# Last joins sooner, first values in two pieces, four decays moved to ScalarE, one transpose moved behind a product

## The chip, the cores and the metric

The kernel runs on one core of a Trainium2 chip. The metric is device time in microseconds (us), the median of three runs. A profiled execution gives a trace besides: every instruction of every engine with its start and duration, and every transfer. TensorE (PE) multiplies matrices, VectorE (DVE), ScalarE (ACT) and GpSimd (POOL) work element by element, SyncE (SP) issues most transfers (DMAs), ACT some. Each engine works through its own list of instructions in order and waits at semaphores for the others.

## The reference

Two layers over 512 latent tokens and 256 context tokens, width 1024: a bidirectional gated delta rule (16 value heads, 8 key heads, chunks of 64 tokens), then attention. The change touches the first layer. Cut to what matters there:

```
kb, vb = kc * bc[..., None], vc * bc[..., None]
a = where(strict, einsum('bhncd,bhnsd->bhncs', kb, kc) * decay, 0)
t_inv = triangular_solve(eye + a, eye, lower=True, unit_diagonal=True)
u = einsum('bhncs,bhnse->bhnce', t_inv, vb)
w = einsum('bhncs,bhnsd->bhncd', t_inv, kb * exp(gc)[..., None])
qk = einsum('bhncd,bhnsd->bhncs', qc, kc) * decay
...
def step(s, xs):                                  # over the chunks, in order
    v_new = u_i - einsum('bhcd,bhde->bhce', w_i, s)
    o = einsum('bhcd,bhde->bhce', qd_i, s) + einsum('bhcs,bhse->bhce', qk_i, v_new)
    s = s * gl_i + einsum('bhcd,bhce->bhde', kd_i, v_new)
    return s, o
...
def finish(o, z):                                 # after the scan
    o = rms_norm(transpose(o, (0, 2, 1, 3)), o_norm_g)
    return (o.reshape(b, l, DN_VAL_DIM) * silu(z)) @ w_out
```

## The kernel before, in words

The tokens lie in six tiles of 128 (t = 0 to 5); a tile holds one chunk for the forward and the mirrored chunk for the backward direction. Three stages matter here.

**Projection stage** (about 140 to 550 us). For each of 40 heads of q, v and z (order `qzzqq...vvzvzvvzzz`: the last are v14, v15, z13, z14, z15) TensorE multiplies in two pieces, 512 and 256 tokens wide (`g512_v15`, `g256_v15`; 24 products each, line 929). A v head is then convolved and gated (VectorE lines 944 and 963), turned by TensorE (`tr_v15`, 461), copied by ScalarE (`vt15`, 994) and stored to memory (`v_d`, 995). Beside it the triangular inverses are made, two tiles at a time: GpSimd solves a 32-wide system column by column (`X0`, `X1`, `X2`, lines 812 and 813), the result is weighed by beta (`weigh`, 817; for the last pair on VectorE), VectorE turns it (`U_4`, `U_5`, 831), and then the halves of each tile are joined: TensorE `pp` (`j_first`, 840), ScalarE `pn` (846), TensorE `pw` (`j_second`, 864), ScalarE copies into `Tt` (852, 871), store to `t_d` (855).

The order of all this on PE, ACT, DVE, POOL and SP is set by a planner (`written_out`): each `Piece` has an engine, a cost, a due time, the pieces it comes after, and the buffers it takes. A piece may start once what it waits for has ended plus a margin (3 us on PE, or the piece's own `slack`); the one that could start first is taken next.

**Recurrence** (about 550 to 730 us). 12 steps (s) of four groups of four heads (p), x = 4s + p. Per x: `ks` (state times keys and queries, 1560), `r` (1563), `pr` (T times r, 1586), `vn` (copy of it, ACT 1588), `vd` (`vn` times a decay, one instruction per head, 1596 on VectorE in step 0, 1598 on ScalarE later), `pq` (1612), `su` (1620), and on VectorE the new state `S` (1632 in step 0, 1634 later) and output `O`. Step 0 starts from a zero state, so it has no `ks`; its `r` is the values tile `cv_0` itself. `pr`, `pq` and `su` have one PSUM buffer each, `ks` two. Each step's tiles (`ck`, `cq`, `cv`, `cT`, `cQK`, `ckt`) are loaded by SP, for step 0 within the projection stage (`first_matrices`, `first_values`). SP's transfers and ACT's share eight semaphores in turn: a transfer is issued only when the eighth before it has landed.

**Output heads** (from about 730 us). Units n = 0 to 31, two groups of three tiles for each of 16 heads: `so` (scaled output, ACT 1690), `pt` (turned, TensorE 1697), gated by z (DVE 1706), `y0` (rounded, ACT 1713) and `y1` (the rest, DVE 1719), product `po` with the split weights (1740). Unit 0 is started within the last x: its third tile (`C`) is turned at x = 47.

Of the kernel before, what the change touches and what calls it, by code (L numbers as in the profile page):

```python
# [86 lines left out]
def backbone(tc, a, out):  # L87
# [713 lines left out]
    def solve_steps(pair):  # L801

        def clear():
            X = Xs[pair] = room["tp" if pair else "even"].tile([P, 2, 32, 32], F32, tag="CDB"[pair], name=f"X{pair}")
            G.memset(X, 0.0)
            G.memset(raw(X.rearrange("p t i j -> p (t i j)"), 0, [[1024, 2], [33, 32]]), 1.0)

        def column(j):
            n, L, X = 31 - j, Ls[pair], Xs[pair]
            tmp = room["tp"].tile([P, 512], F32, tag="tmp", name=f"tmp{j}_{pair}")  # L810
            tv = tmp[:, 0:2 * n * (j + 1)].rearrange("p (t i k) -> p t i k", t=2, i=n)
            G.tensor_tensor(tv, bcast(L[:, :, j + 1:, j], 3, j + 1), bcast(X[:, :, j, 0:j + 1], 2, n), ALU.mult)  # L812
            G.tensor_tensor(X[:, :, j + 1:, 0:j + 1], X[:, :, j + 1:, 0:j + 1], tv, ALU.subtract)  # L813

        def weigh(i):
            X = Xs[pair][:, i]
            (V if pair in (2,) else G).tensor_tensor(X, X, bcast(bball[:, 2 * pair + i], 1, 32), ALU.mult)
# [212 lines left out]

    def first_values():
        opening["v"] = values_tile(0)
        values_loaded(0, opening["v"])

# [292 lines left out]
    for n, (c, h) in enumerate(heads):  # L1327
# [26 lines left out]
        if c == "v":  # L1354
            tu = Piece("PE", 0.6, t0 - 20, head_turned, n, after=si, takes=["tr", "tr"], holds=[("sil", sq_[0])], lands=0.1)
# [42 lines left out]
    for pair in range(3):  # L1398
        first = None
        for j, (cost, f_) in enumerate(solve_steps(pair)):  # L1400
            e = "DVE" if j > 31 and pair in (2,) else "POOL"
            x = Piece(e, 1.22 if e == "DVE" else cost, T0 + (460, 382, 316)[pair], f_, port=1 + (e == "POOL" and 0 < j < 32), after=[turned_["s", 2 * pair], turned_["s", 2 * pair + 1]] + prev, holds=[("L", turned_[2 * pair])] if j < 32 else [], lands=0.1)
            prev = [x]
        solved[pair] = x
    joined = []
    for t in range(NT):
# [4 lines left out]
        U[1].after.append(U[0])  # L1411
        pp = Piece("PE", 1.23, -20, j_first, t, after=U, takes=["gq"], holds=[(u, U[0]), ("mo", mo_of[t])], lands=0.1)
        ne = Piece("ACT", 0.7, due + 4, j_negative, t, after=[pp], takes=["pn"], holds=[("gq", pp)], lands=0.1)
        pw = Piece("PE", 1.23, -20, j_second, t, after=[ne], takes=["gq"], holds=[(u, U[0]), ("pn", ne)], lands=0.1)
        cs = [Piece("ACT", 1.25, due + 10, j_copies, t, b, after=U, takes=[f"Tt{t // 5}"] if b == 0 else (), holds=[(u, U[0])], lands=0.1) for b in range(4)]
# [87 lines left out]
    if True:  # L1503
# [71 lines left out]
        def solve(x):  # L1575
# [14 lines left out]
            if s < 11:  # L1590
                vd = ch.tile([P, 4, P], F32, tag="vd", name=f"vd{x}", bufs=2)
                for c in range(4):
                    h = 4 * p + c
                    el = (elX if c > 1 else elV)[:, visit, t, h:h + 1]
                    if s == 0:
                        V.tensor_scalar(vd[:, c], vn[:, c], el, None, ALU.mult)
# [156 lines left out]
    for x in range(50):  # L1753
# [143 lines left out]
    for n in range(32):  # L1897
# [20 lines left out]
        if n + 2 < 32:  # L1918
            gate_load(n + 2)
            out_scale(n + 2)  # L1920
        if n < 10:
# [632 lines left out]
```

## Time and profile before

| | |
|---|---|
| median of three runs | 1175.51 us (1174.72 to 1175.9) |
| profiled execution, its own time | 1170.3 us |
| its span, first to last instruction | 1168.5 us |
| mean granted TensorE clock | 0.991 |
| TensorE busy | 1124.7 us, 96% |
| VectorE, ScalarE, GpSimd busy | 69%, 62%, 50% |

In a timeline each row is a run of like instructions: start, duration in us, engine, source line, output and inputs, count; in brackets the idle time before it and what ended it. "issue" is idle time for which the profile shows no one that was waited for. Rows of queues (ACTq, SPq) are transfers being issued. A row of windows gives, for a stretch of time, busy time and instructions of each engine, then the granted clock of TensorE, the share of the transfer engines in use and their rate in GB/s. A matrix product of 32-bit values shows as two TensorE records for each one in the program.

### The profile page before, as it was taken

What the parts mean: (1) busy time and instruction counts of PE and PEld (TensorE: products, weight loads), DVE (VectorE), ACT (ScalarE), POOL (GpSimd) and SP (SyncE); (2) the same over time, 40 slices, a digit from 0 to 9 for tenths busy, and PEclk for the clock granted to TensorE, in tenths of its full rate; (3) what the DMA queues carried; (4) which work ended last, traced back from release to release, by engine and by line L of the source; (5) the groups of instructions that cost most, each with busy time, mean ns of one, the idle gap of its engine ahead of it and who ended that gap; (6) DMA issues with size and microseconds to landing.
All of it is one profiled execution on the core that took longest, in us unless ns stands there. A gap on an engine that the chain in (4) does not pass through costs nothing. (4 is left out here: it accounts for less than half of the span.)

```text
span 1168.5 us, 27647 instructions
## 1 busy us (share of the span) xinstructions
PE 1124.7 (96%) x10751; PEld 919.8 (79%) x10751; DVE 801.9 (69%) x1661; ACT 729.8 (62%) x1910; POOL 583.6 (50%) x507
## 2 busy tenths in 40 slices
PE   5999999999999999998899999999999999999996
PEld 2777788888888888887566666788887889999885
DVE  4786565688797888782788888345557476667646
ACT  4445444577777888754589888775753246666731
POOL 0554000159999989910485597556745143130810
PEclk9999999999999999999999999999999999999998
DMA  9577854867748878545988983686844112101323
GB/s 370 201 272 268 293 154 123 231 162 198 200 131 231 243 232 226 167 170 175 310 245 247 282 259 101 196 211 189 255 121 135 37 55 73 37 19 55 109 72 91
DMA packets 116982, 208.73 MB, mean 179 GB/s; under 512 B 12114, under 2 KB 76787, under 8 KB 111475
## 3 DMA queue, kind: packets, MB, share of 16 engines
q1 hardware_dynamic: 96914, 195.32, 54.8%
q10 hardware_dynamic: 19936, 11.64, 3.5%
q8 instruction: 85, 1.39, 0.5%
q14 instruction: 47, 0.38, 0.1%
HBM read 166.16 MB, written 40.67 MB: 177 GB/s over the span
## 5 line engine op out<-in xcount | busy, mean ns | idle before, releaser
L1569 POOL TENSOR_TENSOR S<-S,glb 128x512 f32<-128x512 f32 x80 | 81.7, 1043 | 98.6 <-PE ks L1560 98.3
L1740 PE MATMUL po<-woh,y 128*128 128x512 f32 x384 | 130.5, 404 | 0.0
L1678 POOL TENSOR_TENSOR wol<-wo,woh 128x1024 fp32r<-128x1024 f32 x32 | 77.1, 2411 | 58.7 <-ACT woh L1671 56.3
L813 POOL TENSOR_TENSOR X<-X,tmp 128x62 f32<-128x62 f32 (+15 forms) x93 | 98.0, 1053 | 7.3
L812 POOL TENSOR_TENSOR tmp<-L,X 128x62 f32<-128x62 f32 (+15 forms) x93 | 95.3, 1024 | 6.7
L929 PE MATMUL g_z<-uh,wh_z 128*128 128x512 f32 (+1 forms) x256 | 89.3, 349 | 2.0 <-DVE sil_v L963 2.0
L944 DVE SCALAR_TENSOR_TENSOR acc_v<-g_v,cwv,acc_v 128x510 f32<-128x510 f32 (+3 forms) x128 | 77.9, 613 | 16.4 <-ACT acc_v L936 12.8
L929 PE MATMUL g_v<-uh,wl_v 128*128 128x512 f32 (+1 forms) x256 | 86.2, 337 | 2.0 <-issue 2.0
L929 PE MATMUL g_v<-uh,wh_v 128*128 128x512 f32 (+1 forms) x256 | 88.0, 344 | 0.0
L929 PE MATMUL g_z<-ul,wh_z 128*128 128x512 f32 (+1 forms) x256 | 86.9, 339 | 0.0
L929 PE MATMUL g_z<-uh,wl_z 128*128 128x512 f32 (+1 forms) x256 | 86.7, 338 | 0.0
L929 PE MATMUL g_v<-ul,wh_v 128*128 128x512 f32 (+1 forms) x256 | 86.1, 336 | 0.0
L1740 PEld LDWEIGHTS po<-woh,y 128*128 128x128 f32 x384 | 72.8, 190 | 15.5 <-issue 0.4
L1740 PE MATMUL po<-wol,y 128*128 128x512 f32 x192 | 75.9, 395 | 0.0
L1706 DVE SCALAR_TENSOR_TENSOR pt<-pt,og,z 128x128 f32<-128x128 f32 x96 | 34.4, 358 | 34.6 <-PE pt L1697 32.4
L918 POOL TENSOR_TENSOR wl_z<-w_z,wh_z 128x1024 fp32r<-128x1024 f32 x3 | 7.8, 2611 | 96.3 <-ACT wh_z L915 96.3
L1634 DVE TENSOR_TENSOR S<-su,S 128x512 f32<-128x512 f32 x80 | 51.5, 685 | 5.9 <-PE su L1620 3.7
L1560 PE MATMUL ks<-S,ck 128*64 128x256 f32 x352 | 55.2, 392 | 0.3 <-ACT O L1566 0.2
L929 PEld LDWEIGHTS g_z<-uh,wh_z 128*128 128x128 f32 x256 | 48.8, 191 | 7.9 <-DVE sil_v L963 2.2
L929 PEld LDWEIGHTS g_v<-uh,wl_v 128*128 128x128 f32 x256 | 48.5, 189 | 7.4 <-issue 2.2
L1563 DVE SCALAR_TENSOR_TENSOR r<-ks,negV,cv 128x128 f32<-128x128 f32 x176 | 52.1, 343 | 2.4 <-PE pr L1586 1.3
L929 PEld LDWEIGHTS g_z<-uh,wl_z 128*128 128x128 f32 x256 | 48.9, 191 | 5.4
(453 smaller groups left out, 3341.8 us busy)
## 6 DMA issues: line engine op xcount, KB each, us to landing
aw<-in_ada_late SPq DMA_DIRECT2D x16, 1024.0 KB, 7.6
wo<-in_dn_w_out SPq DMA_DIRECT2D x32, 512.0 KB, 4.1
cv<-v_d SPq DMA_DIRECT2D x24, 512.0 KB, 8.3
aw<-in_ada_first SPq DMA_DIRECT2D x8, 1024.0 KB, 11.0
w_z<-in_dn_w_in SPq DMA_DIRECT2D x16, 512.0 KB, 4.2
w_v<-in_dn_w_in SPq DMA_DIRECT2D x16, 512.0 KB, 4.8
v_d<-vt ACTq DMA_DIRECT2D x16, 384.0 KB, 4.3
cT<-t_d SPq DMA_DIRECT2D x12, 512.0 KB, 7.6
```

The costliest lines, as they stand in the source:

```text
L812: G.tensor_tensor(tv, bcast(L[:, :, j + 1:, j], 3, j + 1), bcast(X[:, :, j, 0:j + 1], 2, n), ALU.mult)
L813: G.tensor_tensor(X[:, :, j + 1:, 0:j + 1], X[:, :, j + 1:, 0:j + 1], tv, ALU.subtract)
L918: E.tensor_tensor(split_w_[n][1], raw_w.pop(n), split_w_[n][0], ALU.subtract)
L929: T.matmul(ps[:, :m], w[:, k], u[:, k, c0:c0 + m], start=k == 0 and n_ == 0, stop=k == KT - 1 and n_ == 2)
L944: V.scalar_tensor_tensor(acc[:, c0 + lo:c0 + hi], ps[:, lo + j - 2:hi + j - 2], cwv[:, j, ct:ct + 1], acc[:, c0 + lo:c0 + hi], ALU.mult, A ...
L1560: T.matmul(ks[r0:r0 + 64, w], kq[w][:, hh, r0:r0 + 64], St[hh][:, d], start=True, stop=True)
L1563: V.scalar_tensor_tensor(r[:, 2 * j + i], ks[:, 0, i], negV[:, visit, t, h:h + 1], v[:, h], ALU.mult, ALU.add)
L1569: G.tensor_tensor(St[hh], St[hh], bcast(g_, 3, P), ALU.mult)
L1634: V.tensor_tensor(St[hh], sj, St[hh], ALU.add)
L1678: G.tensor_tensor(wl, raws.pop(n), halves[n][0], ALU.subtract)
L1706: V.scalar_tensor_tensor(pj, pj, og, raw(z, off, [[st_, 2], [1, 64]]), ALU.mult, ALU.mult)
L1740: T.matmul(acc[nh], y[i][:, j, :], ww[k][:, nh * 512:(nh + 1) * 512], start=h == 0 and x == 0, stop=h == VH - 1 and x == 2)
```

## The change

- `weigh` of the last pair moves from VectorE to GpSimd.
- `first_values` (the load of `cv_0`) becomes two loads: heads 0 to 11, after the stores of v0 to v11, and heads 12 to 15, after the stores of v12 to v15.
- The planner gives `pp` and `pw` of tiles 4 and 5, and the turn of v13, v14 and v15, a margin of 1.2 us in place of 3.
- In step 0 the `vd` of groups 2 and 3 (eight instructions) are made on ScalarE.
- `so` has two buffers; unit 2's `so` stands before unit 1's rounding on ScalarE; unit 0's third tile is turned at x = 48, behind the last `pr`, and gated after it.

```
         def weigh(i):
             X = Xs[pair][:, i]
-            (V if pair in (2,) else G).tensor_tensor(X, X, bcast(bball[:, 2 * pair + i], 1, 32), ALU.mult)
+            G.tensor_tensor(X, X, bcast(bball[:, 2 * pair + i], 1, 32), ALU.mult)
...
-    def values_loaded(t, v):
+    def values_loaded(t, v, h0=0, h1=VH):
...
-            dma(v[hf * 64:hf * 64 + 64], v_d[c // 2, c % 2 * 64:c % 2 * 64 + 64])
+            dma(v[hf * 64:hf * 64 + 64, h0:h1], v_d[c // 2, c % 2 * 64:c % 2 * 64 + 64, h0:h1])
...
+            near = n > 32
+            tu = Piece("PE", 0.6, t0 - 20, head_turned, n, after=si, slack=1.2 if near else None, takes=["tr", "tr"], ...
...
-            e = "DVE" if j > 31 and pair in (2,) else "POOL"
-            x = Piece(e, 1.22 if e == "DVE" else cost, T0 + (460, 382, 316)[pair], f_, ...
+            x = Piece("POOL", cost, T0 + (460, 382, 316)[pair], f_, port=1 + (0 < j < 32), ...
...
-        pp = Piece("PE", 1.23, -20, j_first, t, after=U, takes=["gq"], ...
+        soon = None if t < 4 else 1.2
+        pp = Piece("PE", 1.23, -20, j_first, t, after=U, slack=soon, takes=["gq"], ...
-        pw = Piece("PE", 1.23, -20, j_second, t, after=[ne], takes=["gq"], ...
+        pw = Piece("PE", 1.23, -20, j_second, t, after=[ne], slack=soon, takes=["gq"], ...
...
-    Piece("SP", 1.2, at + 30, first_values, sent=3.0, after=[last["T", 1]] + [last["v", h] for h in range(VH)])
+    fv = []
+    for h0, h1 in ((0, 12), (12, VH)):
+        fv.append(Piece("SP", 1.2, at + 30, first_values, h0, h1, sent=2.4 if h0 == 0 else 0.8, after=[last["T", 1]] + fv + [last["v", h] for h in range(h0, h1)]))
...
-                    if s == 0:
+                    if s == 0 and p < 2:
                         V.tensor_scalar(vd[:, c], vn[:, c], el, None, ALU.mult)
                     else:
                         S.activation(vd[:, c], vn[:, c], AF.Copy, scale=el)
...
-            scaled[n] = fw.tile([P, 3, P], F32, tag="so", name=f"so{h}_{gi}", bufs=1)
+            scaled[n] = fw.tile([P, 3, P], F32, tag="so", name=f"so{h}_{gi}", bufs=2)
...
-        if x == 48:
-            out_gated(0, C)
         if 0 <= x - 2 < 48:
             update(x - 2)
...
             out_load(2)
+        if x == 48:
             out_turn(0, C)
-        if x == 48:
+            out_gated(0, C)
             out_product(0, 0)
...
+        if n == 0:
+            out_scale(n + 2)
...
-            out_scale(n + 2)
+            if n:
+                out_scale(n + 2)
```

What this does to the order is seen at three places. First, TensorE at the end of the projection stage (of each piece of 24 products only the first is shown). Before:

```order
L461 MATMUL tr0_v13_6463<-ident_60,sil_v13_6110 128x128 x4
...
L929 MATMUL g512_z13_6477<-uh_98,wh_z13_6250 128x512
...
L840 MATMUL pp_4_6515<-U_4_6427,mo_4_3475 32x32 x64
L929 MATMUL g256_z13_6583<-uh_98,wh_z13_6250 128x256
...
L461 MATMUL tr0_v14_6623<-ident_60,sil_v14_6391 128x128 x4
...
L929 MATMUL g512_z14_6631<-uh_98,wh_z14_6421 128x512
...
L864 MATMUL pw_4_6686<-pn_4_6612,U_4_6427 32x32 x64
L840 MATMUL pp_5_6753<-U_5_6511,mo_5_3961 32x32 x64
L929 MATMUL g256_z14_6823<-uh_98,wh_z14_6421 128x256
...
L461 MATMUL tr0_v15_6851<-ident_60,sil_v15_6581 128x128 x4
...
L929 MATMUL g512_z15_6859<-uh_98,wh_z15_6609 128x512
...
L864 MATMUL pw_5_6891<-pn_5_6848,U_5_6511 32x32 x64
```

Now:

```order
L840 MATMUL pp_4_6472<-U_4_6399,mo_4_3475 32x32 x64
L461 MATMUL tr0_v13_6539<-ident_60,sil_v13_6110 128x128 x4
...
L929 MATMUL g512_z13_6549<-uh_98,wh_z13_6253 128x512
...
L864 MATMUL pw_4_6592<-pn_4_6574,U_4_6399 32x32 x64
L929 MATMUL g256_z13_6660<-uh_98,wh_z13_6253 128x256
...
L840 MATMUL pp_5_6697<-U_5_6579,mo_5_3961 32x32 x64
L461 MATMUL tr0_v14_6764<-ident_60,sil_v14_6395 128x128 x4
...
L929 MATMUL g512_z14_6788<-uh_98,wh_z14_6426 128x512
...
L864 MATMUL pw_5_6826<-pn_5_6818,U_5_6579 32x32 x64
L929 MATMUL g256_z14_6893<-uh_98,wh_z14_6426 128x256
```

The joins `pp` and `pw` of tiles 4 and 5 stand one to two pieces earlier, and no two of them adjoin; the turns of the v heads keep their places between the products.

Second, SP's transfers from the last weights to step 1's. Before:

```order
L910 DMA w_z14_6212<-in_dn_w_in 128x1024
L897 DMA qk_d_71<-df1_5q_5602 128x4x128
...
L1013 DMA cv_0_6956<-v_d_66 64x2048 x2
L1533 DMA ck_1_7140<-k_d_63 128x1024
L1533 DMA cq_1_7141<-q_d_64 128x1024
L1013 DMA cv_1_7137<-v_d_66 64x2048 x2
L1005 DMA cT_1_7136<-t_d_70 128x1024
L1006 DMA cQK_1_7138<-qk_d_71 128x1024
L1007 DMA ckt_1_7139<-kt_d_65 128x1024
```

Now:

```order
L910 DMA w_z14_6212<-in_dn_w_in 128x1024
L1013 DMA cv_0_6216<-v_d_66 64x1536 x2
L897 DMA qk_d_71<-df1_5q_5602 128x4x128
...
L1537 DMA ck_1_7142<-k_d_63 128x1024
L1537 DMA cq_1_7143<-q_d_64 128x1024
L1005 DMA cT_1_7138<-t_d_70 128x1024
L1013 DMA cv_0_6216<-v_d_66 64x512 x2
L1013 DMA cv_1_7139<-v_d_66 64x2048 x2
L1006 DMA cQK_1_7140<-qk_d_71 128x1024
L1007 DMA ckt_1_7141<-kt_d_65 128x1024
```

Three quarters of step 0's values are now loaded right behind z14's weights; the last quarter comes after three of step 1's loads. By the turn of the eight semaphores, `ckt_1` waited for the store of tile 5's `Tt` before; now `cv_1` does.

Third, TensorE where the recurrence ends. Before:

```order
L1586 MATMUL pr46_9925<-r46_9851,cT_11_9704 64x128 x8
L1612 MATMUL pq45_9938<-vn45_9881,cQK_11_9706 64x128 x8
L1697 MATMUL pt0_9896<-ident_60,so0_0_9804 128x128
L1586 MATMUL pr47_9953<-r47_9901,cT_11_9704 64x128 x8
L1612 MATMUL pq46_9965<-vn46_9934,cQK_11_9706 64x128 x8
```

Now:

```order
L1590 MATMUL pr46_9927<-r46_9853,cT_11_9706 64x128 x8
L1616 MATMUL pq45_9940<-vn45_9883,cQK_11_9708 64x128 x8
L1590 MATMUL pr47_9954<-r47_9903,cT_11_9706 64x128 x8
L1616 MATMUL pq46_9965<-vn46_9936,cQK_11_9708 64x128 x8
L1701 MATMUL pt0_9898<-ident_60,so0_0_9806 128x128
```

The turn of unit 0's third tile now stands behind the last `pr` and the `pq` after it.

More of the change, by code (lines that the diff above doesn't have):

```diff
@@ L1029, in first_matrices, with first_values @@
         matrices_loaded(0, 0, *opening["m"])
-    def first_values():
-        opening["v"] = values_tile(0)
-        values_loaded(0, opening["v"])
+    def first_values(h0, h1):
+        if h0 == 0:
+            opening["v"] = values_tile(0)
+        values_loaded(0, opening["v"], h0, h1)
     class Buffers:
@@ L1354, in backbone @@
         if c == "v":
-            tu = Piece("PE", 0.6, t0 - 20, head_turned, n, after=si, takes=["tr", "tr"], holds=[("sil", sq_[0])], lands=0.1)
+            near = n > 32
+            tu = Piece("PE", 0.6, t0 - 20, head_turned, n, after=si, slack=1.2 if near else None, takes=["tr", "tr"], holds=[("sil", sq_[0])], lands=0.1)
             kept(("v", h), Piece("ACT", 1.0, e + 12, head_copied, n, after=[tu], takes=["tok"], holds=[("tr", tu), ("tr", tu)], sent=1.15, far=1.4))
@@ L1400, in backbone @@
         for j, (cost, f_) in enumerate(solve_steps(pair)):
-            e = "DVE" if j > 31 and pair in (2,) else "POOL"
-            x = Piece(e, 1.22 if e == "DVE" else cost, T0 + (460, 382, 316)[pair], f_, port=1 + (e == "POOL" and 0 < j < 32), after=[turned_["s", 2 * pair], turned_["s", 2 * pair + 1]] + prev, holds=[("L", turned_[2 * pair])] if j < 32 else [], lands=0.1)
+            x = Piece("POOL", cost, T0 + (460, 382, 316)[pair], f_, port=1 + (0 < j < 32), after=[turned_["s", 2 * pair], turned_["s", 2 * pair + 1]] + prev, holds=[("L", turned_[2 * pair])] if j < 32 else [], lands=0.1)
             prev = [x]
```

4 lines of the change are left out of this document (2 added, 2 removed).

## The prediction

> **What bounds the kernel.** I read the page's first part, then the list of what TensorE waited for, then windows for its clock. The list has the line of each wait, whom it waited for, the total in us, how often, and the longest.
>
> ```profile
> PE 1124.7 (96%) x10751; PEld 919.8 (79%) x10751; DVE 801.9 (69%) x1661; ACT 729.8 (62%) x1910; POOL 583.6 (50%) x507
> PE pt L1697 <- ACT so L1690: 2.7, 2, 2.0
> PE su L1620 <- DVE S L1632: 2.5, 2, 1.9
> PE pp L840 <- issue: 1.9, 1, 1.9
> 343.76 0.50 PE L929 MATMUL g_z<-uh,wh_z 128*128 128x512 f32 x1 [1.95 <-DVE sil_v L963]
> 345.30:348.70 3.40, 3.40 (x10) 2.63 (x9) 3.40 (x5) 3.37 (x11) 2.70 (x3) 0.50 1.05 270
> 553.50:556.90 3.40, 3.06 (x48) 2.53 (x51) 1.86 (x9) 1.46 (x3) 0.00 (x0) 0.50 1.04 341
> 731.00:734.40 3.40, 3.40 (x22) 2.34 (x22) 0.89 (x2) 2.19 (x6) 2.28 (x2) 0.50 0.58 159
> ```
>
> TensorE sets the time: 96% busy. Its work is the same after the change, so only its waits and its slow stretches can give anything. The three quoted from the list, `pt`, `su` and `pp`, stand where the change works; a fourth, for `cv`, follows below. The row at 343.76 is one that it doesn't touch. The windows show three stretches of 3.4 us at half the granted clock (third number from the right). Two of them follow waits that the change touches. A half-clock stretch with TensorE busy costs 1.7 us.
>
> **The opening of the recurrence** (values in two pieces, decays on ScalarE). TensorE's rows, then those of the others there:
>
> ```profile
> 550.48 0.43 PE L1586 MATMUL pr<-cv,cT 64*64 64x128 f32 x2
> 552.48 0.66 PE L1586 MATMUL pr<-cv,cT 64*64 64x128 f32 x14 [1.57 <-DMA cv<-v_d]
> 553.84 1.13 PE L1586 MATMUL pr<-cv,cT 64*64 64x128 f32 x16 [0.69 <-ACT vn L1588]
> 558.82 1.09 PE L1620 MATMUL su<-vd,ckt 64*64 64x256 f32 x16 [0.65 <-DVE S L1632]
> 568.75 1.09 PE L1620 MATMUL su<-vd,ckt 64*64 64x256 f32 x16 [1.86 <-DVE S L1632]
> 569.89 0.65 PE L1560 MATMUL ks<-S,ck 128*64 128x256 f32 x4
> 571.77 0.67 PE L1586 MATMUL pr<-r,cT 64*64 64x128 f32 x16
> 551.46 0.33 ACTq L1002 DMA_DIRECT2D z_d<-sil_z  x1
> 553.20 0.58 ACT L1588 COPY vn<-pr 128x512 f32<-128x512 f32 x1 [2.23 <-PE pr L1586]
> 564.88 1.33 DVE L1596 TENSOR_SCALAR vd<-vn,elV 128x128 f32<-128x128 f32 x2 [1.23 <-ACT vn L1588]
> 567.32 1.28 DVE L1632 COPY S<-su 128x512 f32<-128x512 f32 x2
> 718.04 0.69 ACT L1598 ACTIVATE vd<-vn,elV 128x128 f32<-128x128 f32 x2
> ```
>
> From the start of the first `pr` to that of the third group of `ks` (569.89) are 19.41 us. Now the new course, from zero at that start.
>
> The first piece of `cv_0` has long been there, so the 1.57 us go. The next limit is ScalarE: `vn` stands behind the issue of z15's store, which ends at 551.79, 1.3 us after the start. So `vn` runs from 1.35 to 1.95, and the second `pr` starts at 2.0 in place of 553.84 − 550.48 = 3.36. Of the two waits of 1.57 and 0.69 one of 1.5 remains.
>
> From there, at full clock, the steps are the work itself, by the gaps between starts in the rows: `pr` and `pq` about 0.47 each, `su` 0.97, four `ks` 1.88 (569.89 to 571.77). Second `pr`, `pq` and `su` end at 3.9, the next `pr` and `pq` at 4.85. The second `su` waits for the state copies, 1.28 behind the first `su`: 5.3, a wait of 0.45. `su` and `ks` bring 8.15; `pr`, `pq`, `su`, `ks` 11.95; `pr`, `pq`, `su` 13.85, if the last `su` does not wait. It waited 1.86 us because four decays took 2.4 us on VectorE (564.88 to 567.32, beside GpSimd's first state decays) and the copies came behind them. On ScalarE two take 0.69, so four some 1.3; the fourth `vn` is ready at 9.4, its decays at 10.7, and the copies on VectorE now run right behind the third `su`, done at 11.4. The last `su` is due at 12.9. ScalarE's added 1.3 us for each group push copies of `O` back by as much, to 11.2, where the fourth `pq` needs them at 12.45.
>
> Gain: 19.41 − 13.85 = **5.5**, of which 1.7 is the half-clock stretch at 553.5. Bounds: 2 if the clock still falls and step 1's loads come a few us late, 5.8 if nothing waits. `cv_1` must land before the first `pr` of step 1, 11.9 after the start.
>
> **The earlier joins.** These rows are TensorE's:
>
> ```profile
> 442.74 1.47 PE L840 MATMUL pp<-U,mo 32*32 32x32 f32 x128
> 445.30 0.77 PE L461 MATMUL tr_v<-ident,sil_v 128*128 128x128 f32 x5 [0.84 <-issue]
> 507.37 0.39 PE L929 MATMUL g_v<-uh,wl_v 128*128 128x256 f32 x1 [1.98 <-issue]
> 532.56 1.25 PE L864 MATMUL pw<-pn,U 32*32 32x32 f32 x126
> 536.82 0.25 PE L840 MATMUL pp<-U,mo 32*32 32x32 f32 x5 [1.93 <-issue]
> q8 instruction: 85, 1.39, 0.5%
> 505.40:508.80 3.40, 1.43 (x7) 1.22 (x8) 2.03 (x3) 1.60 (x4) 0.00 (x0) 1.00 1.01 414
> ```
>
> The wait of 1.93 us ends in the last five records of a `pp` that directly follows a `pw`. The 85 instruction transfers fit TensorE's 2 × 10751 instructions, some 253 in each. One join is 128 products and 128 weight loads, a whole transfer's worth in 1.3 us; two in a row outrun the supply. Counted in instructions (a piece of products 48 with its weight loads, a turn 12, a join 256), the stalls at 507 and 536 lie 1024 apart, four times 256, so I read both as a transfer not yet in. After the change joins stand 4 to 7 us apart. On the same count only the end of the last `pw` is near an edge, 2.4 us behind the edge before it, where a refill took 2.6 us (442.74 to 445.30) to some 3.3: a wait of 0 to 0.9. Gain 1.0 to 1.9, I take **1.5**.
>
> The joins also bring tile 5's store forward:
>
> ```profile
> 549.91 0.34 ACTq L855 DMA_DIRECT2D t_d<-Tt  x1
> 561.43 0.32 SPq L1007 DMA_DIRECT2D ckt<-kt_d  x1
> 547.53 2.34 ACT L871 COPY Tt<-pw 32x512 f32<-32x512 f32 x4 [0.63 <-PE pw L864]
> cv<-v_d SPq DMA_DIRECT2D x8, 512.0 KB, 7.6
> ```
>
> Tile 5's `pw` now follows the piece that tile 4's followed (532.56), with two more joins ahead: 532.56 + 2.5 + 1.3 for itself + 2.4 of copies, 538.8 in place of 549.9. Before, `ckt_1` was held until that store landed, 11.5 us. Now `cv_1` is held by it, until 550 at worst, some 546 if a quieter queue takes the 7.6 of a load, and lands 7.6 later, at 554 to 558. Its deadline is about 560 (TensorE reaches the recurrence 1.5 us sooner, at 549, and 11.9 follow). Behind it stand `cQK_1`, `ckt_1` and `cq_2`, with deadlines 4 us later and more. The second piece of `cv_0` waits as before for v15's store and has 8 us. So I cost this at nothing; the cover is 2 to 6 us, and each us beyond costs one.
>
> **The first output head.**
>
> ```profile
> 729.58 0.33 PE L1697 MATMUL pt<-ident,so 128*128 128x128 f32 x1 [1.98 <-ACT so L1690]
> 729.84 0.67 PE L1586 MATMUL pr<-r,cT 64*64 64x128 f32 x16
> 736.08 0.49 PE L1697 MATMUL pt<-ident,so 128*128 128x128 f32 x3
> 738.67 0.91 PE L1697 MATMUL pt<-ident,so 128*128 128x128 f32 x3 [0.70 <-ACT so L1690]
> 739.33 0.49 PE L1740 MATMUL po<-woh,y 128*128 128x512 f32 x1
> 728.61 0.62 ACT L1588 COPY vn<-pr 128x512 f32<-128x512 f32 x1
> 738.35 0.56 DVE L1719 TENSOR_TENSOR y<-pt,y 128x384 fp32r<-128x384 f32 x1 [0.59 <-ACT y L1713]
> ```
>
> The last `pr` needs the copy `vn`, done at 729.23, so it can start at 729.27 in place of 729.84: the wait shrinks from 1.98 to about 1.65. `pr`, `pq` and the turn, 1.25 by the gaps between starts, bring 730.5. Six products take 1.6 (from the turn's three records at 736.08 to 737.97, where the wait of 0.70 begins, are 1.89, of which 0.25 the turn). Two groups and one `pq` of 0.5 bring unit 1's turn to its end at 734.3. Six more and unit 2's turn end at 736.5, and unit 1's product waits for `y1`, 738.91 − 736.57 = 2.35 behind its turn: 736.65. It started at 739.33: gain **2.7**, 1.7 of it clock. If the clock falls all the same, 1.0.
>
> **The clock.** The three half-clock stretches lie 61 × 3.413 and 52 × 3.413 us apart. On that grid, the one before each holds 1.9 us or more of idle TensorE; the waits at 507, 536 and 568 put at most 1.65 into one and left the clock alone. The new waits of 1.5 and 1.65 are at or below that. The Trainium skill ("TensorE: Matmul & The Clock Gate", section "What's actually happening") has the same free-running window of 3413 ns, but lets the clock fall after a whole idle window; this trace disagrees, with falls behind waits of 2 us. By that rule the stretches would have another cause and stay; that is the third rival.
>
> **Costed at nothing, or little.** Weighing moves to GpSimd, which is idle from 500.42 on:
>
> ```profile
> L817 POOL TENSOR_TENSOR X<-X,bball x4: 2390/2410/3412, 327.4 to 419.2; 128x1024 f32<-128x1024 f32 x4
> 513.83 2.23 DVE L831 STREAM_TRANSPOSE U<-X 128x1024 f32<-128x1024 f32 x1
> ```
>
> Two take 4.8 us, 6.8 at worst, so to 507 at most; VectorE is freed of 2.4. The second turn of tile 4 ended at 516.06 and now can at about 512.3; `pp` wants it at 515.9. Cover 3.6 us. The turns of v13 to v15 keep their places, so their margin does nothing. The early load, 0.75 MB at about 492, comes ahead of a stretch in which transfers are full (414 GB/s, share 1.01); it can lengthen the stall at 507 by up to 0.75 / 0.414 = 1.8. I take a cost of **0.3**.
>
> **Sum.** 5.5 + 1.5 + 2.7 − 0.3 = 9.4 on the profiled execution, 1170.3 to 1160.9. The runs have a median of 1175.51, 5.2 above it, which the trace doesn't explain. Of the 9.4, 3.4 are clock. A 2 us wait puts 1.75 us or more into one window of a grid that runs free only in about half of the positions, so I count half of the 3.4: 7.7. **1175.5 − 7.7 = 1167.8.**
>
> **Rivals.**
> - *The stalls move* (0.16). Instruction supply stalls elsewhere, since TensorE gets on faster there, and 1.5 and 1.65 us still halve the clock. For it: no margin on the grid. Against it: 536's stall needs two joins in a row. 9.4 − 1.5 − 3.4 = 4.5: 1171.0.
> - *Transfers take the place* (0.12). `cv_1` lands 5 us late and step 1 waits: 7.7 − 5 = 2.7: 1172.8.
> - *The clock falls for another reason* (0.06). 9.4 − 3.4 = 6.0: 1169.5.
> - *The waits only change their names* (0.07): ScalarE's and VectorE's queues bind in the opening, the head gains nothing: 1175.
> - *Slower* (0.05). The hold of `cv_1` on tile 5's store: SP issues in order, so if that store, 1 MB beside three loads, lands 22 us after issue rather than 11.5, `cv_1` and six loads behind it come 10 us late and step 1 stands. From there on it outweighs 7.7: 1178. Against it: no landing in the trace comes near that.
> - My forecast (0.54): 1164.5 to 1170.5.
>
> Less than 0.2% (2.35 us) cannot be told from no change. Faster takes the first, the third, my own and most of the second: 0.86. Within 0.2%: 0.09. Slower: 0.05. Range 1163.5 to 1172.8: below, all of the clock and 0.9 for the stall; above, the second rival.
>
> **What would show it.** Right: no wait of the first `pr` for `cv`, one of 1.5 for `vn`; no 1.8 us wait of `su`; no issue stall within a `pp`; tile 5's `Tt` stored near 538; one half-clock stretch behind 500 us at most; the last `pr` before its turn, with a wait of about 1.65. Wrong: waits for `cv`, `cQK` or `ckt` in step 1, `g` products that wait for `U` or `sil`, or a longer stall near 507.

## The result, and the profile after

| | median | beside it, before | ratio, 95% interval |
|---|---|---|---|
| the changed kernel | 1163.29 us | 1175.12 us | 0.9914 (0.9891 to 0.9937) |
| predicted | 1167.8 us | 1175.5 us | 0.9934 (range of the forecast 0.9898 to 0.9977) |

The changed kernel is faster by 0.6 to 1.1%. The ratio in the first row is not the plain quotient of the two medians, of four executions each: that is 0.9899, inside the same interval. Two later timings gave 0.9945 (0.9925 to 0.9965) and 0.9922 (0.9893 to 0.9952), so the predicted 0.9934 lies within what was measured. Executions of one kernel spread widely here, those of before from 1167 to 1179 us. The 5.2 us that its trace didn't explain are such a spread, at both ends: the profiled execution (1170.3) was a fast one, and the first median (1175.5, of three) lies above those of the later and longer timings (1172.3, 1173.4 and 1173.9). One execution, of the kernel called "`vn` first" below, ran at a granted clock of 0.75 and took 1392 us; no figure here counts it.

The profiled execution of the changed kernel took 1162.5 us, its span is 1160.7 in place of 1168.5. First its page's busy row, and from the list of what TensorE waited for the rows that the change touches (total in us, how often, longest):

```profile
PE 1122.1 (97%) x10751; PEld 917.8 (79%) x10751; DVE 796.3 (69%) x1651; ACT 735.2 (63%) x1918; POOL 589.1 (51%) x509
PE pr L1590 <- ACT vn L1592: 3.0, 2, 1.7
PE g_v L929 <- issue: 1.3, 1, 1.3
PE pw L864 <- issue: 1.0, 1, 1.0
PE su L1624 <- DVE S L1636: 0.7, 1, 0.7
```

The waits of `pr` for the values, of the last `su` (1.9), of `pp` on the instruction supply (1.9) and of `pt` for `so` (2.7 in all) are gone. `pr` waits for `vn` twice, 1.33 and 1.68 (1.5 and 1.65 were forecast). New is a wait at the end of a `pw`. TensorE is busy 2.6 us less with the same work, which fits the two half-clock stretches that are gone. Its rows in TensorE's timeline, stage by stage:

```profile
506.40 0.38 PE L929 MATMUL g_v<-uh,wl_v 128*128 128x256 f32 x1 [1.27 <-issue]
534.76 1.22 PE L864 MATMUL pw<-pn,U 32*32 32x32 f32 x121
537.00 0.26 PE L864 MATMUL pw<-pn,U 32*32 32x32 f32 x7 [1.02 <-issue]
...
549.27 0.67 PE L1590 MATMUL pr<-cv,cT 64*64 64x128 f32 x16
551.27 0.67 PE L1590 MATMUL pr<-cv,cT 64*64 64x128 f32 x16 [1.33 <-ACT vn L1592]
554.84 1.09 PE L1624 MATMUL su<-vd,ckt 64*64 64x256 f32 x16 [0.73 <-DVE S L1636]
563.71 0.65 PE L1564 MATMUL ks<-S,ck 128*64 128x256 f32 x4
...
567.31 1.08 PE L1624 MATMUL su<-vd,ckt 64*64 64x256 f32 x12 [0.19 <-issue]
612.67 0.32 PE L1590 MATMUL pr<-r,cT 64*64 64x128 f32 x2 [0.29 <-issue]
...
721.41 0.67 PE L1590 MATMUL pr<-r,cT 64*64 64x128 f32 x16
724.20 0.67 PE L1590 MATMUL pr<-r,cT 64*64 64x128 f32 x16 [1.68 <-ACT vn L1592]
731.43 0.50 PE L1744 MATMUL po<-woh,y 128*128 128x512 f32 x1
```

From the first `pr` to the third group of `ks` (563.71) it is now 14.44 us (19.41 before). From the last but one `pr` to unit 1's first product (731.43) it is 10.02 (12.83 before: 726.50 to 739.33). And a window view around the two places where before had half the clock: in each row the third number from the right is the granted clock.

```profile
552.60:556.00 3.40, 2.67 (x62) 1.85 (x56) 2.07 (x6) 2.66 (x7) 0.00 (x0) 1.00 0.95 235
724.80:728.20 3.40, 3.40 (x46) 2.41 (x42) 1.63 (x4) 2.22 (x6) 2.30 (x1) 1.00 0.35 134
```

Both are at full clock. The difference of the two traces, 7.8 us, taken apart by the same instructions in both:

| stretch | before | changed | gain | predicted |
|---|---|---|---|---|
| up to the first `pr` | 550.48 | 549.27 | 1.2 | 1.2 (1.5 − 0.3) |
| first `pr` to third `ks` group | 19.41 | 14.44 | 5.0 | 5.5 |
| from there to the last but one `pr` | 156.61 | 157.70 | −1.1 | 0 |
| to unit 1's first product | 12.83 | 10.02 | 2.8 | 2.7 |
| to the end | 429.17 | 429.27 | −0.1 | 0 |

### The profile page after: what moved, and what is told of

It reads as the page before. It is cut to its first block, busy times and chain, and to the rows that moved or that the text cites. A ratio compares the mean times of both kernels' runs of the same rounds, so it can differ in the third digit from the quotient of the medians.

```text
span 1160.7 us, 27663 instructions
## 1 busy us (share of the span) xinstructions
PE 1122.1 (97%) x10751; PEld 917.8 (79%) x10751; DVE 796.3 (69%) x1651; ACT 735.2 (63%) x1918; POOL 589.1 (51%) x509
```

## The experiments

Two questions were open: does each part bring what its term says, and is the account of the causes (late values, instruction transfers, clock) the right one? For each kernel the same marks are read. "Opening" is first `pr` to third `ks` group, "head" the last but one `pr` to unit 1's first product, "stalls" TensorE's waits on the instruction supply ("issue") of 0.3 us or more between 430 and 625 us, and the last column the half-clock stretches between 500 and 750 us.

| kernel | median | ratio to before | opening | head | stalls | half clock |
|---|---|---|---|---|---|---|
| before | 1172.3 to 1175.1 (four timings) | 1 | 19.41 | 12.83 | 0.8, 2.0, 1.9 | 2 |
| changed | 1163.29 | 0.9914 (0.9891 to 0.9937) | 14.44 | 10.02 | 0.5, 1.3, 1.0 | 0 |
| values alone | 1172.97 | 0.9998 (0.9979 to 1.0017) | 14.13 | 12.92 | 0.6, 1.1, 1.9, 1.8 | 2 |
| decays alone | 1173.95 | 1.0018 (0.9996 to 1.0040) | 17.22 | 11.31 | 0.4, 1.9, 1.9, 1.1 | 2 |
| head alone | 1170.39 | 0.9984 (0.9968 to 1.0001) | 19.13 | 10.00 | 1.8, 1.9 | 1 |
| changed without joins | 1167.14 | 0.9963 (0.9943 to 0.9984) | 14.42 | 10.00 | 0.7, 2.0, 2.2, 0.7, 2.1 | 2 |
| changed, again | 1166.84 | 0.9945 (0.9925 to 0.9965) | 14.70 | 10.02 | 1.4, 0.9, 0.3, 1.6 | 0 |
| changed without decays | 1162.86 | 0.9916 (0.9889 to 0.9942) | 14.16 | 9.99 | 0.7, 1.7, 0.7 | 1 |
| shifted by 192 | 1162.10 | 0.9909 (0.9882 to 0.9935) | 14.15 | 11.48 | none | 1 |
| shifted by 48 | 1163.52 | 0.9914 (0.9889 to 0.9939) | 15.39 | 10.02 | 1.6 | 1 |
| `vn` first | 1163.30 | 0.9918 (0.9887 to 0.9950) | 14.71 | 9.39 | 0.8, 1.2, 1.0, 0.3 | 0 |
| combined | 1162.96 | 0.9905 (0.9870 to 0.9939) | 17.65 | 9.40 | none | 0 |
| changed, third time | 1164.53 | 0.9922 (0.9893 to 0.9952) | 14.44 | 9.99 | 0.6, 1.3, 1.0, 1.6 | 0 |
| changed without joins, again | 1167.73 | 0.9962 (0.9938 to 0.9985) | 14.26 | 10.00 | 1.5, 1.9, 0.5, 2.1 | 1 |

A half-clock stretch adds some 1.7 us to whatever stretch it falls into, so a mark read from a trace and a median over executions are two different things here. The first says what a part does, the second what it is worth. Medians from different rows are not to be set against each other, since they were not all timed beside the same executions of before; the ratios are.

**The values alone.**

```
-    Piece("SP", 1.2, at + 30, first_values, sent=3.0, after=[last["T", 1]] + [last["v", h] for h in range(VH)])
+    fv = []
+    for h0, h1 in ((0, 12), (12, VH)):
+        fv.append(Piece("SP", 1.2, at + 30, first_values, h0, h1, ...
```

> The kernel before with one edit, step 0's values in two pieces; no other instruction moves. My account: the wait for the values (1.57) goes, one of 1.3 for vn stands in its place, the long wait of su (1.86) stays. From the first pr to the third group of ks it was 19.41 us: without the wait 18.1, and 16.4 if the half-clock stretch at 553 goes with it because no grid window holds 1.9 us of idle TensorE any more. So 3.0 us less on the trace. Rival (the clock falls for another reason): 18.1 and still a half-clock stretch there, 1.4 us less. The stall near 507 tells what the earlier load does to it: longer by up to 1.8 (my cost of 0.3), or shorter, as the whole change's trace has it (1.27).

In its trace the opening fell to 14.13, more than either account had: the 1.86 us of the last `su` went too, without the decays being touched. TensorE's rows, then VectorE's:

```profile
551.74 0.67 PE L1589 MATMUL pr<-cv,cT 64*64 64x128 f32 x16
553.73 0.67 PE L1589 MATMUL pr<-cv,cT 64*64 64x128 f32 x16 [1.32 <-ACT vn L1591]
564.90 1.04 PE L1623 MATMUL su<-vd,ckt 64*64 64x256 f32 x16
565.87 0.65 PE L1563 MATMUL ks<-S,ck 128*64 128x256 f32 x4
```

```profile
559.67 1.26 DVE L1566 SCALAR_TENSOR_TENSOR r<-ks,negV,cv 128x128 f32<-128x128 f32 x4
562.16 0.48 DVE L1599 TENSOR_SCALAR vd<-vn,elV 128x128 f32<-128x128 f32 x2 [1.23 <-ACT vn L1591]
562.56 0.48 DVE L1599 TENSOR_SCALAR vd<-vn,elX 128x128 f32<-128x128 f32 x2
```

VectorE makes `r` of step 1 without a wait, and the four decays take 0.9 us. In before's trace VectorE stood idle 1.25 us ahead of `r`, and the decays took 2.4. The row of `r` there, two of ScalarE's rows behind it, and the last row of the view of the values tile (`cv`), which has the time from issue to landing:

```profile
562.53 1.13 DVE L1563 SCALAR_TENSOR_TENSOR r<-ks,negV,cv 128x128 f32<-128x128 f32 x4 [1.25 <-PE pr L1586]
563.23 1.14 ACT L1566 ACTIVATE O<-ks,egV 128x128 f32<-128x128 f32 x4 [4.31 <-DVE r L1563]
564.26 0.58 ACT L1588 COPY vn<-pr 128x512 f32<-128x512 f32 x1
```

```profile
DMA to landing us min/median/max: 5.3/7.4/14.0
```

The row names `pr`, but the second half of step 1's values was issued at some 548.5, and 548.5 + 14.0 is 562.5, where `r` starts. So step 1's values were late before. How that reached the decays is in ScalarE's rows: it stood idle 4.31 us until `r` let it make the outputs `O` of step 1, and the copy `vn` for which the decays wait stands behind `O` in its queue. The state copies stand behind the decays on VectorE. With the earlier load of step 0's values, step 1's landed 9.7 us after their issue in place of 14.0, and the whole chain came in time. Yet the median did not move. On this trace 1.3 us are left of the 5.3: the recurrence behind the opening took 2.7 more, with a new stall of 1.8 us at 586.4, and the first `pr` came 1.3 later, behind a half-clock stretch at 538 that followed the stall in `pp`. A second such stretch, at 729, followed the wait of `pt`, as in before.

**The decays alone.**

```
-                    if s == 0:
+                    if s == 0 and p < 2:
```

> The kernel before with one edit, step 0's decays of the third and fourth group on ScalarE. My account: the wait of 1.86 of the last su in step 0 goes, and with it the 0.2 of a pq; nothing else moves, the half-clock stretch at 553 stays, since the waits of 1.57 and 0.69 stay. First pr to third ks 17.5 in place of 19.41: about 2 us less. Rival (waits only change their names): ScalarE's queue makes pq or the next pr wait instead, 19 and no gain.

The wait of 1.86 went and the opening is 17.22, as the account had it (17.5). Here `r` is late with its cause named:

```profile
563.11 1.13 DVE L1563 SCALAR_TENSOR_TENSOR r<-ks,negV,cv 128x128 f32<-128x128 f32 x4 [0.87 <-DMA cv<-v_d]
```

With the decays on ScalarE a late `r` no longer holds up the state copies. The median does not show it (1.0018, if anything slower).

**The head alone.**

```
-        if x == 48:
-            out_gated(0, C)
...
+        if x == 48:
             out_turn(0, C)
-        if x == 48:
+            out_gated(0, C)
...
+        if n == 0:
+            out_scale(n + 2)
```

> The kernel before with one edit, the first output head (third tile turned behind the last pr, two buffers of so, unit 2's so first). My account: from the last but one pr to unit 1's first product 10.0 in place of 12.83, with a wait of the last pr of 1.65 and no half-clock stretch there: 2.8 us less. Rival (the clock falls for another reason, or 1.65 us is enough): the half-clock stretch stays, 11.7, 1.1 us less.

10.00, with the wait of 1.68 and no half-clock stretch: as the account had it. In the median it is 0.9984, with an interval that just reaches 1. In "decays alone" the unchanged head, with the same wait of 1.98, took 11.31 in place of 12.83, since the clock did not fall there in that execution: so of the 2.8 us, 1.5 are clock, which comes or not, and the other 1.3 are saved either way.

**The joins** (the changed kernel without them).

```
-            G.tensor_tensor(X, X, bcast(bball[:, 2 * pair + i], 1, 32), ALU.mult)
+            (V if pair in (2,) else G).tensor_tensor(X, X, bcast(bball[:, 2 * pair + i], 1, 32), ALU.mult)
...
-        soon = None if t < 4 else 1.2
```

> The changed kernel with its weighing and its margins for joins and turns undone; TensorE's order in the projection stage is then that of before, with pw of tile 4 directly ahead of pp of tile 5. My account: the stall of 1.9 in that pp is back in place of the 1.0 at the end of the last pw, less some 0.5 of seams between joins and products: 0.5 us slower than the changed kernel on the trace. If the stall near 507 is 1.3 as in the changed kernel, the earlier load made it shorter; if 2.0, the moved weighing did. The recurrence's opening and the head as in the changed kernel (14.4 and 10.0), no half-clock stretch behind 500 us unless the 1.9 falls into one window. Rival (the joins bring nothing): same time as the changed kernel within 0.3 us.

```profile
537.03 0.32 PE L840 MATMUL pp<-U,mo 32*32 32x32 f32 x5 [2.24 <-issue]
588.12 0.37 PE L1615 MATMUL pq<-vn,cQK 64*64 64x128 f32 x1 [2.08 <-issue]
```

The stall in `pp` is back, and the clock fell behind it. A second one of 2.08 stands in the recurrence, and the clock fell there too. The stall near 507 was 1.97 in this trace and 1.46 in that of the second timing, and 1.2 to 1.7 with the joins moved, so its size doesn't tell which part of the change acts on it. Timed again beside the changed kernel:

> The changed kernel without its weighing and margins, now beside the changed kernel on one chip. Account A (the joins bring what the traces of the stalls say): the stall of 1.9 to 2.2 in pp of tile 5 in place of 0.9 to 1.0 behind pw, less 0.5 of seams, plus the clock, which 1.9 halves more often than 1.0: 1 to 2 us slower than the changed kernel. Account B (worth nothing): within 0.7 us, as the first timing had it (0.9963 against 0.9945 on another chip).

> The changed kernel again, the yardstick for the others of this call: ratio to before 0.993 (the two values so far are 0.9914 and 0.9945).

1167.73 against 1164.53 us, 3.2 us slower, with the same two stalls (1.93, 2.08). The single intervals overlap, so the 1 to 2 us of account A are not excluded; but both timings of this kernel gave 0.9962 to 0.9963, the three of the changed kernel 0.9914 to 0.9945, which is 2 to 6 us. The joins are probably worth more than their 1.5, and that they bring nothing is unlikely. Before's order of the projection stage has a stall of 1.1 to 2.1 in the recurrence at the same instruction (of `pq`, 585.8 to 588.1) in all four traces whose opening was shortened; with the joins separated no trace has it, but some have 0.2 to 1.6 at 567 to 569.

**The changed kernel again.**

> The changed kernel itself, timed once more beside the others on one chip. Before's executions spread over 10 us (1167 to 1178 in 31 of them), so its median and the changed kernel's are only comparable side by side. My account: by the traces the whole change gives 7.8 us and the three parts without the joins some 5; about 1163 to 1165 where before has 1172. If the joins bring nothing beyond the parts, 1167 like the kernel without them.

1166.84, at the upper end: taken alone, this timing says that the joins bring nothing, as the kernel without them had 1167.14 on another chip; the pair on one chip, above, says otherwise. Its trace agrees with the first (span 1160.5).

**Without the decays.**

```
-                    if s == 0 and p < 2:
+                    if s == 0:
```

> The changed kernel with step 0's decays of the third and fourth group back on VectorE. In the trace with the values alone the 1.86 us wait of the last su had gone without this edit: VectorE no longer stood at r, which waits for step 1's values, when the decays were due. Account A (the wait came from step 1's late values): first pr to third ks 14.1 to 14.5 as in the changed kernel, same time within the noise. Account B (as predicted, four decays on VectorE are too slow): the wait of 1.86 is back, 16.3, 1.9 us slower.

Account A held: opening 14.16. The median, 1162.86, is even 4 us below that of the changed kernel beside it (1166.84), with intervals that overlap. So here the moved decays brought nothing. That isn't the whole of it, as the combined kernel below shows.

**Shifted instructions.**

```
             arows[q] = pa.tile([P, 512], F32, tag="gq", name=f"pa{q}")
+            for _ in range(48 if q == 0 else 0):
+                T.matmul(arows[q][0:64, 0:1], square[:, 0:64], ones, start=True, stop=True)
```

> The changed kernel with 48 tiny products (64 x 1, 192 instructions) ahead of TensorE's first one, where it waits 9.6 us for VectorE anyway; they are overwritten. Nothing else moves. Account A (issue stalls are instruction transfers, at edges every 256 instructions of TensorE's list, and last as long as a refill takes beyond the work between two edges): every edge falls 192 instructions earlier in the program, and by the count none falls where a whole join lies between two edges: the stalls near 445, 506 and 537 (0.5, 1.3, 1.0) go or shrink to under 0.4 each, 2 to 2.8 us less on the trace. Account B (the stalls belong to those places, by the transfers' load or the joins themselves): they stay.

> The same with 12 products (48 instructions). Account A: the edges fall 48 instructions earlier; the one near 506 moves into the turn behind pw of tile 3 (near 501.5) with a whole join between it and the edge before it and full transfers, so a stall of 3 to 4 us there; one of some 1 us in or behind pp of tile 5 (near 528); the one at 445 and the one at the end of the last pw go. In sum 4 to 5 us of stalls in place of 2.8: 1.5 to 2 us slower than the changed kernel, more where the stall of 3 to 4 us halves the clock. Account B: as the changed kernel.

The first kernel has 48 of these products, the second 12. In the first all stalls between 430 and 625 us are gone, without one instruction of that stretch being moved. In the second, those at 445, 506 and 537 are gone and one of 1.57 stands behind the `pp` of tile 5, where the count had put it. The stall of 3 to 4 us near 501 that the account expected there didn't come, and the kernel wasn't slower (1163.52): I had taken a refill time of 5.5 us. Rows of the second kernel, then one of the first, then two windows of the second:

```profile
504.68 0.50 PE L931 MATMUL g_v<-uh,wh_v 128*128 128x512 f32 x1 [1.42 <-DVE sil_z L963]
527.83 1.08 PE L463 MATMUL tr_v<-ident,sil_v 128*128 128x128 f32 x6 [1.57 <-issue]
```

```profile
506.75 0.50 PE L931 MATMUL g_v<-uh,wh_v 128*128 128x512 f32 x1 [1.42 <-DVE sil_z L963]
```

```profile
524.92:528.33 3.41, 1.84 (x134) 1.68 (x134) 2.22 (x10) 1.55 (x4) 0.00 (x0) 1.00 0.80 314
528.33:531.74 3.41, 3.41 (x12) 2.73 (x11) 0.00 (x0) 2.74 (x6) 0.00 (x0) 0.50 1.02 317
```

So the stalls belong to the count of TensorE's instructions (account A). One near 506 and one near 537 stand in all eleven traces without these products, and in none of the three with them. They are not gone from the kernel altogether: the first kernel has one of 0.40 at 655.9, where the changed kernel has none. And both show what the stall near 506 had covered: the first product behind it waits for VectorE's `sil_z`, 1.42 us. Taking the stall away uncovers that wait, so the place is worth nothing. The first kernel's head took 11.48, because the wait of 1.68 brought half clock this time. Its trace is 1159.5, its median 1162.10 against 1166.84 for the changed kernel timed beside it, with intervals that overlap.

**`vn` first.**

```
-        if x == 47:
-            out_cast(0, AB)
         if 0 <= x - 1 < 48:
             solve(x - 1)
         if x == 47:
+            out_cast(0, AB)
+            for f_ in later:
+                f_()
```

`later` holds the scaled outputs `o` of x = 47 and their sum, which stood ahead of `solve`.

> The changed kernel with one more edit: for the last x, ScalarE copies vn of x = 46 ahead of the four scaled outputs o of x = 47 (and of unit 0's rounding), behind which it stood. My account of the 1.68 us that the last pr still waits: vn stands in ScalarE's queue behind o, which waits for VectorE's r (2.2 us idle before it). With vn first it ends by 722.7 on the changed kernel's time scale, r by 722.65, so the last pr starts at 722.8 in place of 724.2: wait 0.3 to 0.5, last but one pr to unit 1's first product 8.7 in place of 10.0, and no half-clock stretch can follow there (it does in some executions behind 1.68). 1.3 us less on a trace without that stretch, about 2 in the median. Rival: the products wait for y instead (10.0, no gain).

```profile
720.37 0.67 PE L1600 MATMUL pr<-r,cT 64*64 64x128 f32 x16 [0.32 <-ACT vn L1602]
721.70 0.67 PE L1626 MATMUL pq<-vn,cQK 64*64 64x128 f32 x16 [0.66 <-DVE O L1640]
```

The wait fell to 0.32 as expected, so the place in ScalarE's queue was its cause. But half of the gain went into a new wait: the next `pq` waits 0.66 for VectorE, which still had to take `O` out of its one buffer. Head 9.39 in place of 10.02, not 8.7. The ratio (0.9918 beside 0.9922) shows nothing of it.

**Combined**, meant as a version that beats both kernels.

> The changed kernel with vn first as above, the 48 tiny products ahead (edges of the instruction transfers 192 earlier), and step 0's decays back on VectorE. Parts by their traces: 1.3 for vn first; no issue stalls from 430 to 625 us where the changed kernel has 0.5, 1.3, 1.0 and up to 1.9 in the recurrence, of which the one at 506 only uncovers a wait of 1.4 for VectorE; decays 0. A trace of 1157 to 1159 where the changed kernel has 1160.6, a median of 1159 to 1161.

No stalls, a head of 9.40, and an opening of 17.65: the wait of 1.86 is back. Two of VectorE's rows and one of TensorE's:

```profile
559.42 1.13 DVE L1569 SCALAR_TENSOR_TENSOR r<-ks,negV,cv 128x128 f32<-128x128 f32 x4 [2.26 <-DMA cv<-v_d]
561.77 1.33 DVE L1612 TENSOR_SCALAR vd<-vn,elV 128x128 f32<-128x128 f32 x2 [1.23 <-ACT vn L1604]
```

```profile
565.65 1.09 PE L1636 MATMUL su<-vd,ckt 64*64 64x256 f32 x16 [1.86 <-DVE S L1648]
```

In this execution step 1's values came late again (`r` waited 2.26 us for them), and with the decays on VectorE behind `r` that costs the 1.86. In "shifted by 48" `r` waited 1.76 for them too, but the decays were on ScalarE: no wait of 1.86, opening 15.39. So by the traces the moved decays are an insurance: nothing where the values come in time, some 2 us where they come late. No median shows it. The combined kernel beats before (0.9905), but its median of 1162.96 misses the 1159 to 1161 that I expected, and against the changed kernel timed beside it (0.9922) it isn't told apart.

## Why the prediction was right, point by point

**The sum** was right, 1167.8 against 0.9914 × 1175.5 = 1165.4 by the first timing and 1166.3 to 1169.0 by the other two. That it came so close is luck, since two errors offset each other. The waits gave less: 7.8 us on the trace less 3.4 of clock are 4.4, where I had 6.0. The clock gave more: I counted half of the 3.4. Over the executions of the second and third timing of the changed kernel the mean granted clock was 0.9928, over those of before beside them 0.9899, and 0.0029 of 1165 us are 3.4 us: on average two half-clock stretches fewer, not one. They need not be the two of before's trace, which is all that I counted: where the grid lies otherwise, the stall in `pp` halves the clock, as it did in four of the six traces that have it, and that stall goes with the change too.

**The opening** (5.5 predicted, 5.0 measured). The first `pr` did not wait for the values, and the second started 2.00 behind it, as forecast, behind the store of z15. The next `su` waited 0.73 where I had 0.45, and the third `su` ran 0.3 long (a stall of 0.3 on the instruction supply, where the second trace of this kernel names it). The step that failed is the cause of the 1.86 us: "It waited 1.86 us because four decays took 2.4 us on VectorE (564.88 to 567.32, beside GpSimd's first state decays)". The 2.4 us were there, but as a consequence. `r` waited for step 1's late values, `O` and `vn` on ScalarE came late behind it, and so the decays began late enough to run beside GpSimd. Two of them then take 1.33 us in place of 0.48. One decay of the pair and GpSimd's two state decays in before's trace:

```profile
565.08 1.13 DVE L1596 TENSOR_SCALAR vd<-vn,elV 128x128 f32<-128x128 f32 x1
565.08 2.04 POOL L1569 TENSOR_TENSOR S<-S,glb 128x512 f32<-128x512 f32 x2 [1.97 <-PE ks L1560]
```

GpSimd's two take 1.02 each. The decay starts with the first of them, at 565.08, and ends at 566.21, just behind it. Begun in time, as with the values alone, the four took 0.9 on VectorE, done 0.2 us ahead of GpSimd's next state decay, and nothing waited. On the slow decay the Trainium skill ("SBUF — State Buffer", section "SBUF: two separate sides") says that VectorE, in some of its modes, and GpSimd share a port pair, which one of them holds for a whole instruction while the other blocks; the 0.48 against 1.33 agrees. I had seen the slow decays, not asked why they stood where they stood, though their row names the wait of 1.23 for `vn`, and put on ScalarE's account what the values piece brings.

**The joins** (1.5 predicted, 0.3 on the trace, 2 to 6 in the medians). The two stalls that I had read as late instruction transfers are that: moving the count moved them. The wait of 0 to 0.9 at the end of the last `pw` came, with 1.02. But the agreement of the table's first row, 1.2 and 1.2, is luck. Of the measured 1.2, 0.3 stood before any join had moved, and 0.7 is the stall near 507, which shrank where I had a cost of 0.3. The joins' own term is 1.93 less 1.02, and less some 0.6 that four separated joins cost more than three groups of them: from the product behind the first stall to the first `pr` it took 42.6 us less 1.0 of stall, before 42.9 less 1.9. So the term was too high by 0.6 for the seams, which I had put at nothing, and by 0.6 for the wait left behind `pw`, 1.02 where I had taken 0.4. And I stopped counting at the recurrence, where the traces without the joins lose up to 2.1 us more.

**The stalls move** was a rival with 0.16, and it came true in part, beside the forecast and not in its place: stalls of 0.2 and 0.3 in the recurrence's rows, which cost 1.1 us of its time (two steps of 4.6 and 4.5 us in place of 3.8, less 0.5 that before lost there), up to 1.6 in other executions, up to 2.1 with before's joins. Before and "head alone", the two traces with an opening of 19 us, have none there. I take it that their waits of 1.3 to 1.9 let the supply get ahead; no run shows that by itself. It would explain part of why the values alone gave 5.3 us on the opening and nothing in the median, and why the joins count for more than their own stall.

**The head** (2.7 predicted, 2.8 measured): the steps held, with a wait of 1.68 where 1.65 was predicted.

**Transfers take the place**, and the rival on the slower side (the hold of step 1's values on tile 5's store). That store was issued at 539.7 (538.8 predicted) and landed at 545.2 (some 546 predicted), but it was not the hold. The stores of tile 5 and of v15 on ACT's queue, and the values on SP's, two transfers for the last quarter of step 0's and two for step 1's:

```profile
539.70 0.34 ACTq L855 DMA_DIRECT2D t_d<-Tt  x1
541.69 0.37 ACTq L995 DMA_DIRECT2D v_d<-vt  x1
546.37 2.41 SPq L1013 DMA_DIRECT2D cv<-v_d  x4
```

SP issues them in the order of its list, and the last quarter of step 0's values, which stands ahead of step 1's, had to wait for v15's store. That landed at 546.2, and the quarter went out 0.1 behind it; step 1's values followed at 547.5 and 548.2 and landed at 555.8, within the 554 to 558 forecast, by luck. I had treated the two waits as if neither stood behind the other. The deadline was wrong too: I took the first `pr` of step 1, at about 560, but `r` needs the values first, and it ran at 557.2. In "shifted by 48" and "combined" v15's store landed at 548.1 and 548.9, step 1's values at 558.7 and 559.3, ahead of that deadline, and `r` still waited 1.8 and 2.3 us for them; the opening was 1.0 and 3.2 longer than the changed kernel's, the second with the decays on VectorE. So the cover was 1.4 us in this trace and nothing in those two, where I had 2 to 6.

**The clock.** Both stretches went in this trace. The step said of the waits that "at most 1.65" in one window left the clock alone and that the new ones "of 1.5 and 1.65 are at or below that". Laid on the 3.413 us grid of each trace's own half-clock stretches, all windows of the fourteen traces from 60 us on say the same of a clock that was full before: the nineteen in which TensorE idled 1.73 us or more, up to 3.16, were each followed by half clock, those with 1.56 or less never, and 1.68 whole in one window left it alone in the changed kernel and in three others. Half a window is 1.71. But it is no sharp edge:

```profile
720.53:723.94 3.41, 1.73 (x42) 1.21 (x35) 1.52 (x5) 2.70 (x8) 3.19 (x3) 1.00 0.45 105
723.94:727.35 3.41, 3.41 (x23) 2.11 (x21) 1.08 (x3) 2.59 (x8) 1.77 (x2) 0.51 0.41 113
```

These are windows of "shifted by 192": there the same wait of 1.68 halved the clock, and in "shifted by 48" one of 1.57. So the step held for 1.65 in most traces and not in all. The new waits lie right under the edge, before's of 1.9 to 2.0 over it, and whether such a wait falls whole into one window is left to the grid. The rule of the Trainium skill ("TensorE: Matmul & The Clock Gate", section "What's actually happening"), that the clock falls after an idle window, fails here if that means a window without any work: half of one is enough. Its free-running grid fits.

What the runs leave open: which part of the median's gain belongs to which part of the change. The parts alone give 0.9998, 1.0018 and 0.9984, three parts together 0.9963, all of it 0.9914 to 0.9945. That they are worth more together than one by one is what stalls that move and a clock that falls by chance would do, but no run shows how much of it each of the two makes. What set the size of the stall near 507 stays open too.

## What to carry to other kernels

When a wait goes, look at what it gave time to: here stalls on the instruction supply came up in the next stage, and a part that saved 5 us at its place saved nothing in the median on its own. Follow a late instruction back through every queue on its way before moving it elsewhere: the decays were slow only since they were late, they were late by a copy on another engine, and that by a transfer. In an ordered queue of transfers, look at what stands ahead of the one that matters, and take its deadline from the first instruction on any engine that reads it. And where executions of one kernel differ by more than the change is worth, take the mechanism from the marks in the trace and the worth from medians side by side, never from one profile.

## What the runs showed of the hardware

- TensorE's instructions come in transfers of some 256. Where TensorE reaches the end of one before the next is in, it stands for 0.2 to 2.2 us, and the profile calls it "issue". 48 tiny products far ahead, in idle time, took away all such stalls between 430 and 625 us, and one of 0.40 stood behind that stretch, at 655.9; with 12 of them one stall stood, at another place. I had not expected that so little decides it.
- The clock halves for a window of 3.41 us (for two of them twice, near 890 us) after one in which TensorE idles for about half of it: 1.73 us and more in one window did it nineteen times of nineteen, 1.56 and less never, 1.57 and 1.68 once each while eight other windows with 1.63 to 1.69 did not. What decides in that strip isn't settled.
- A pair of VectorE's decays (128x128) took 0.48 us alone and 1.33 beside GpSimd's state decay; the slow one of the two starts with GpSimd's instruction and ends just behind it.
